# Three 32-byte pads that shift which half of a 64-byte line matmul operands start in

## The chip, the cores and the metric

The kernel runs on one core of a Trainium2 chip. The metric is the device time of one launch in microseconds (us). Three runs of the kernel before took 3115.22, 3119.87 and 3125.04 us; their median is 3119.87 us. The profile shows one more execution, engine by engine: PE is TensorE's matmuls, PEld its weight loads, DVE is VectorE, ACT is ScalarE, POOL is GpSimd, SP issues most DMAs.

## The reference, cut to what matters

One transformer block on 2048 tokens of width 1024, all in float32. The block modulates a layer norm of x, projects it to 6144 columns, runs a convolution branch and a bidirectional retention branch with 4 heads, mixes the two, projects again and normalises. Then come 16 experts, each of which picks 256 tokens:

```python
xe = jax.vmap(lambda hb, ib: hb[ib])(h, idx)
he = jax.nn.silu(jnp.einsum('becd,edf->becf', xe, w_gate)) * jnp.einsum('becd,edf->becf', xe, w_up)
ye = jnp.einsum('becf,efd->becd', he, w_down) * gates[..., None].astype(h.dtype)
```

The matrices `w_gate`, `w_up` and `w_down` are 1024 x 1024 for each expert, so the experts hold most of the arithmetic and most of the weights.

## The kernel before

Nearly every product is made by `mm3` (lines 86 to 89). An operand is kept as two float32r tiles, a high part and a remainder, which `split` (lines 77 to 84) writes: ACT copies the source to the high part (line 80) and DVE subtracts it from the source (line 81). `mm3` then issues three matmuls, high by high, high by low and low by high. The first argument of a matmul streams through TensorE as the moving operand, the second is loaded as the stationary operand. In the trace a matmul is named out<-moving,stationary; so `mm<-xeT,sg` has the tokens `xeT` moving and the expert's weights `sg` stationary, and `mm<-sd,heT` has the weights `sd` moving and the activations `heT` stationary. A matmul with an activation moving has 256 columns here, one with a weight moving mostly 512.

SBUF tiles live in pools that lie one behind the other in each partition, in the order in which the pools are opened: `const`, `wp`, `sm`, and behind them pools that come and go with the stages (`ip`, `hp`, `cvp`, `evp` for the input projections, `rpa` and `rp` for retention and output projection, `ep` for the experts). Within a pool the slots lie in the order in which their tags are first used, and each slot is rounded up to a multiple of 32 bytes. So a slot starts either at byte 0 or at byte 32 of a 64-byte line. `wp` has four `raw` slots (DMA destinations) and 24 slots with tag `w`, all of 4096 bytes; `wp` starts at byte 20480, so all of them start at 0. The pools behind `sm` start at 136960, also at 0. In `ep` come `g2r` (4096 bytes), `kio` (672 bytes, an odd number of 32s) and `idx` (128 bytes), so `heT`, both `xeT` slots, the 2 KB work tiles and `ye` start at 32, while `xe` starts at 0.

Which operand starts where, in the kernel before (moving, stationary):

| matmuls (out<-moving,stationary) | what | moving at | stationary at |
|---|---|---|---|
| `mm<-xeT,sg` | experts, gate and up, 256 columns | 32 | 0 |
| `mm<-sd,heT` | experts, down, 512 columns | 0 | 32 |
| `mm<-hT,sU` | input projection U, 256 columns | 0 | 0 |
| `mm<-sK,hT` and with sQ, sV, sG, sGA, sGB | the other input projections, 512 columns | 0 | 0 |
| `ro<-sw,oTs`, `mm<-sw,yTs`, `mm<-sw,ats` | output projections, 512 columns | 0 | 0 |
| `o<-SS,qws`, `o<-vsr,ats`, `u<-vs,kd`, `ub<-vsr,kd` | retention, 256 columns | 0 | 0 |

`make_hT` (line 256) puts the transposed tokens `hT` of the pairs 0, 1, 5 and 6 in the `hp` pool and those of the pairs 2, 3, 4, 7 and of the context in `w` slots (line 258). In retention `kTs`, `qTs` and `qws` lie in `w` slots, `SS`, `vsr`, `oTs`, `yTs` and nearly all `ats` in `rpa` and `rp`. The order of the work is written out by hand in program order; SP's queue issues the weight loads, and a `raw` slot is loaded again when both of its splits have read it.

Of the kernel before, what the change touches and what calls it, by code (L numbers as in the profile page):

```python
# [9 lines left out]
F32 = mybir.dt.float32  # L10
# [8 lines left out]
DRAM = bass.MemoryType.DRAM  # L19

P = 128
# [7 lines left out]
CAP = 256  # L29
# [13 lines left out]
def body(ctx: ExitStack, tc: tile.TileContext, x, ctxt, cc, w_ada, b_row, b_col, w_in, conv_w, conv_b,  # L43
# [3 lines left out]
    V, A, G, T = nc.vector, nc.scalar, nc.gpsimd, nc.tensor  # L47
# [4 lines left out]
    pp = ctx.enter_context(tc.tile_pool(name="pp", bufs=1, space=PSUM))  # L52
    dr = ctx.enter_context(tc.tile_pool(name="dr", bufs=1, space=DRAM))

    def dram(name, shape, dt=F32):
        return dr.tile(shape, dt, name=name, tag=name)

# [30 lines left out]
        T.matmul(ps, s[0], m[1], start=False, stop=False)  # L88
        return T.matmul(ps, s[1], m[0], start=False, stop=stop_)  # L89

# [1 line left out]
    def cload(name, src, shape, dt=F32, eng=None):  # L92
        t = const.tile(shape, dt, name=name)
        (eng or nc.gpsimd).dma_start(t, src)
# [25 lines left out]
    CB, SB, GB, WB = dect[:, 5], dect[:, 6], dect[:, 7], dect[:, 8:10]  # L120
    wr = const.tile([P, KD, 32], F32, name="wr")

# [1 line left out]
    d_kr = [dram(f"d_kr{t}", [P, 512]) for t in range(NT)]  # L124
    d_kT = [dram(f"d_kT{t}", [P, 512]) for t in range(NT)]
    d_qT = [dram(f"d_qT{t}", [P, 512]) for t in range(NT)]
# [15 lines left out]
    pows, exps = [None], [None]  # L142

    def ln_scale(src, nchunk, heads=1, eps=EPS, fin=True):
        """src [P, nchunk*w] -> rstd, -mean*rstd as [P, heads]"""
        w = src.shape[-1] // nchunk
        n = nchunk // heads
        st = sm.tile([P, nchunk, 6], F32, name="st", tag="st", bufs=4)
        for i in range(nchunk):
            V.bn_stats(st[:, i], src[:, i * w:(i + 1) * w])  # L150
        mv = sm.tile([P, heads, 2], F32, name="mv", tag="mv", bufs=4)
        for h in range(heads):
            V.bn_aggr(mv[:, h], st[:, h * n:(h + 1) * n])
        if not fin:
            rs = sm.tile([P, 1], F32, name="rs1", tag="rs1", bufs=4)
            V.tensor_scalar(rs, mv[:, 0, 1:2], eps, None, op0=ALU.add)  # L156
            pows[0] = G.tensor_tensor(rs, rs, mhalf[:, :1], ALU.pow)  # L157
            return rs, mv
        return ln_fin(mv, heads, eps)
# [9 lines left out]
        for j in range(4):  # L169
            T.transpose(ps[:, j * P:(j + 1) * P], src[:, (k0 + j) * P:(k0 + j + 1) * P], ident)  # L170

    # ======================= input projections =======================
    inp = ExitStack()
    ip = inp.enter_context(tc.tile_pool(name="ip", bufs=1))
    hp_ = inp.enter_context(tc.tile_pool(name="hp", bufs=1))
# [74 lines left out]
    ring = {}  # L250

    def make_hT(pid, src, t0, which):
        """pair of token tiles: modulated LN, transposed, split"""
        tag = "h" if pid in (0, 1, 5, 6) else "w"
        tiles = []
        for kk in range(4):
            if tag == "h":
                tiles.append(hp_.tile([P, 2, 2, 2 * P], F32R, name=f"hT{pid}_{kk}", tag="h", bufs=8))
            else:
                tiles.append(wslot(f"hT{pid}_{kk}", [P, 2, 2, 2 * P]))  # L260
        for t in range(2):
            xt = ip.tile([P, D], F32, name="xt", tag="t4k", bufs=3)
            nc.sync.dma_start(xt, src[(t0 + t) * P:(t0 + t + 1) * P])
            rs = ln_scale(xt, 2)
            A.activation(xt, xt, AF.Identity, scale=rs[:, 0], bias=rs[:, 1])
            for hf in range(2):
                ps = tr_ps()
                transpose4(xt, hf * 4, ps)
                hf32 = t2k("hf32")
                for j in range(4):  # L270
                    k = hf * 4 + j
                    cj = slice(j * P, (j + 1) * P)
                    if j % 2:
                        A.activation(hf32[:, cj], ps[:, cj], AF.Identity,
                                     scale=modc[:, 1, k, which:which + 1], bias=modc[:, 0, k, which:which + 1])
                    else:
                        V.tensor_scalar(hf32[:, cj], ps[:, cj],
                                        modc[:, 1, k, which:which + 1], modc[:, 0, k, which:which + 1],
                                        op0=ALU.mult, op1=ALU.add)
                for q in range(2):  # L280
                    dst = tiles[hf * 2 + q]
                    split(dst[:, :, 0, t * P:(t + 1) * P], dst[:, :, 1, t * P:(t + 1) * P],
                          hf32[:, q * 256:(q + 1) * 256].rearrange("p (k c) -> p k c", k=2))
        ring[pid] = tiles
# [5 lines left out]
        return tl[:, k % 2, 0, t * P:(t + 1) * P], tl[:, k % 2, 1, t * P:(t + 1) * P]  # L290

    def load_w(src, ks, scale=None, res=None):
        """rows of 128 of [n, 1024] -> slabs[half][k]"""
        res = [[], []] if res is None else res
        for k in ks:
            r = raw("rw", [P, D])
            nc.sync.dma_start(r, src[k * P:(k + 1) * P])
            for n in range(2):
                s = wslot("sw", [P, 2, 512])
                split(s[:, 0], s[:, 1], r[:, n * 512:(n + 1) * 512], scale=None if scale is None else scale[:, k:k + 1])  # L300
                res[n].append((s[:, 0], s[:, 1]))
        return res
# [25 lines left out]
    st = {}  # L328

    def rope(ps, t, kq):  # L330
        """ps [P, 512] psum -> rotated f32 pieces written to dst"""
        cs = ip.tile([P, 2, 64], F32, name="cs", tag="cs", bufs=2)
        nc.scalar.dma_start(cs, k_rope[kq, t])
        a = t2k("ra")
        b = t2k("rb")
        pv = ps.rearrange("p (h d) -> p h d", d=64)
        V.tensor_tensor(a.rearrange("p (h d) -> p h d", d=64), pv, cs[:, 0:1].to_broadcast([P, 8, 64]), ALU.mult)
        V.tensor_tensor(b.rearrange("p (h d) -> p h d", d=64), pv, cs[:, 1:2].to_broadcast([P, 8, 64]), ALU.mult)
        a4 = a.rearrange("p (h e d) -> p h e d", e=2, d=64)
        b4 = b.rearrange("p (h e d) -> p h e d", e=2, d=64)  # L340
        return a4, b4
# [243 lines left out]
    inp.close()  # L585


    # ======================= retention =======================
    ret = ExitStack()
    rpa = ret.enter_context(tc.tile_pool(name="rpa", bufs=1))  # L590
    rp = ret.enter_context(tc.tile_pool(name="rp", bufs=1))
# [16 lines left out]
        return s  # L608

    def T_split(src, name):  # L610
        """[P, 1024] token-major -> transposed hi/lo tiles"""
        tl = []
        for hf in range(2):
            ps = tr_ps()
            transpose4(src, hf * 4, ps)
            s = hlT(name)
            split(s[:, 0], s[:, 1], ps)
            tl.append(s)
        return lambda k: (tl[k // 4][:, 0, (k % 4) * P:(k % 4 + 1) * P], tl[k // 4][:, 1, (k % 4) * P:(k % 4 + 1) * P])
# [99 lines left out]
    w_conv_s = load_w(w_conv, range(4))  # L719
    ret_b(0, T_split(prev, "oTs"))  # L720

    # ======================= output projection, LN, router =======================
    def row_const(name, src, off=0, plus1=False):
        if name == "l1b":
            t = rpa.tile([P, D], F32, name=name, tag="tabr", bufs=1)
# [109 lines left out]
                hTs = []  # L835
    ret.close()

    # ======================= expert choice: top CAP tokens of each expert =======================
    moe = ExitStack()
    ep = moe.enter_context(tc.tile_pool(name="ep", bufs=1))  # L840
    def tk(name, w, dt=F32, bufs=1):
# [10 lines left out]
    nc.scalar.dma_start(kio, k_iota)  # L852
    iota16, tokid, blk, iota128 = kio[:, 0:16], kio[:, 16:32], kio[:, 32:40], kio[:, 40:168]
    idx = ep.tile([P, NE * 2], U32, name="idx")

    def gu_slabs(src, f2, ahead=False):
        res = [[], []]
# [30 lines left out]
    for i in range(14, -1, -1):  # L888
        cnt = tk("cnt", 3, BF16, 2)
        for j in range(3):  # L890
            junk = e2k("junk")
            junk = junk[:, :128].bitcast(BF16) if i >= 8 else junk[:, :256]
            V.tensor_scalar(junk, seg16 if i >= 8 else seg, cand[:, j + 1:j + 2].bitcast(F32), 0.0,
                            op0=ALU.is_ge, op1=ALU.add, accum_out=cnt[:, j:j + 1])
        pc = u_ps("cnt")
        cmm = T.matmul(pc[:, 0:3], sameb, cnt, start=True, stop=True)
        if i < 14:
            with tc.issue_after(cmm.ins):
                pump(1, g2fill)
        hits = tk("hits", 3, F32, 2)  # L900
        dig = tk("dig", 1, F32, 2)
        if i > 0:
            nx = tk("nx", 4, I32, 2)
            V.tensor_tensor(nx, cand[:, 0:1].to_broadcast([P, 4]), digit[:, i - 1], ALU.bitwise_or)
        else:
            nx = cand[:, 0:1].to_broadcast([P, 4])
        V.tensor_scalar(hits, pc[:, 0:3], CAP - 0.5, 0.0, op0=ALU.is_ge, op1=ALU.add, accum_out=dig)
        cand = tk("cand", 4, I32, 2)
        if i >= 4:
            # at most 24 significant bits: exact in float32  # L910
            V.scalar_tensor_tensor(cand, dig.to_broadcast([P, 4]), float(1 << 2 * i), nx, op0=ALU.mult, op1=ALU.add)
        else:
            digi = tk("digi", 1, I32, 2)
            V.tensor_scalar(digi, dig, float(1 << 2 * i), None, op0=ALU.mult)
            V.tensor_tensor(cand, digi.to_broadcast([P, 4]), nx, ALU.bitwise_or)
# [61 lines left out]
        g0 = 2 if gq == 0 else 0  # L977
        nc.sync.dma_start(idx[:, gq * 8 + g0:(gq + 1) * 8], d_idx.rearrange("(h g p) o -> h p (g o)", h=4, p=P)[gq][:, g0:])

    # list of expert 0, in the layout that its gathers read  # L980
    pin0 = pin.rearrange("p (a s e) -> p a s e", a=2, s=8)[:, :, :, 0]
    pt = tk("pt", 32, I32)
    V.tensor_scalar(pt[:, 0:16].rearrange("p (s a) -> p a s", a=2), pin0, P - 1, None, op0=ALU.bitwise_and)
# [23 lines left out]
    V.tensor_copy(pabf, pab)  # L1007


    # ======================= experts =======================  # L1010
    def x_prep(e):
        xeT = ep.tile([P, KD, 2, 256], F32R, name="xeT", tag="xeT", bufs=2)
        gts = []
# [138 lines left out]
    moe.close()  # L1152


# [1 line left out]
def layout(**inp):  # L1156
    f=lambda n: np.ascontiguousarray(inp[n])
    w_in=inp['w_in'][0]
# [60 lines left out]
```

## Time and profile before

| | before |
|---|---|
| median of 3 runs | 3119.87 us (3115.22 to 3125.04) |
| profiled execution, span | 3120.2 us |
| PE busy | 2992.0 us, 96% of the span |
| DVE busy | 2142.9 us, 69% |
| ACT busy | 1170.9 us, 38% |
| mean granted TensorE clock | 0.979 |

Of the profiled execution the records give the span from the first to the last instruction; no time outside it is recorded. A matmul's duration in the records runs from its issue to its modelled end and overlaps the next one, so the cost of a matmul in a dense stream is read from the distance between the starts of neighbours, here called the spacing, and not from its duration.

### The profile page before, as it was taken

Reading aid. Unit: us, or ns where it says so; the run is one execution under the profiler, and the core shown is the slowest. Engines: PE = TensorE matmul, PEld = TensorE weight load, DVE = VectorE, ACT = ScalarE, POOL = GpSimd, SP = SyncE. Lnnn points to the kernel's source line nnn. Section 1 sums busy time; section 2 is a strip of 40 time slices with the busy share of each in tenths; the row PEclk is TensorE's granted clock in tenths of the full one; section 3 lists DMA queues with packets and bytes.
Section 4 is the critical chain, followed back from the end, with each engine's and each line's share of the span. In section 5 each row is a group of like instructions: output and inputs, shape, how many; then the busy total and the mean of one; then the engine's idle time right before and its main releaser. Section 6 shows DMA issues by size and latency. Waiting matters only on the chain.

```text
span 3120.2 us, 47124 instructions
## 1 busy us (share of the span) xinstructions
PE 2992.0 (96%) x17897; PEld 2599.5 (83%) x17897; DVE 2142.9 (69%) x3964; ACT 1170.9 (38%) x2182; POOL 338.2 (11%) x294
## 2 busy tenths in 40 slices
PE   6999999999999999899999995999999999999897
PEld 3988877789888887788888881999999999998886
DVE  4366777452669985888877777566666666588686
ACT  4323123252232233555421112555555555444342
POOL 2100000000000000111101114100000000011131
PEclk8999999999999999899999996999999999999998
DMA  6244355332442334666754444666766666588774
GB/s 238 82 147 169 135 172 174 121 109 87 170 180 90 118 117 143 208 205 210 238 198 151 145 139 158 199 204 213 212 218 215 210 211 211 175 274 270 243 257 162
DMA packets 195043, 560.22 MB, mean 180 GB/s; under 512 B 29064, under 2 KB 44328, under 8 KB 194816
## 3 DMA queue, kind: packets, MB, share of 16 engines
q1 hardware_dynamic: 174880, 503.68, 48.4%
q0 software_dynamic: 13456, 47.84, 6.0%
q10 hardware_dynamic: 6480, 5.70, 0.6%
q8 instruction: 140, 2.29, 0.3%
q14 instruction: 87, 0.71, 0.1%
HBM read 429.24 MB, written 127.89 MB: 179 GB/s over the span
## 4 chain that ended last, share of the span: by engine, by line
PE 85%; DMA 6%; DVE 4%; issue 2%; ACT 2%; POOL 1%; SPq 0%; POOLq 0%; DVEq 0%; ACTq 0%
PE mm L87 24%; PE mm L89 23%; PE mm L88 23%; PE tr L170 2%; PE ro L87 2%; PE ro L89 2%; PE ro L88 2%; DMA rg<-w_gate 1%; DMA d_acc<-ye,idx 1%; DMA rg<-w_up 1%; PE ada L206 1%; PE o L87 1%; PE o L88 1%; PE o L89 1%; DVE sd L81 1%
## 5 line engine op out<-in xcount | busy, mean ns | idle before, releaser
L89 PE MATMUL mm<-xeT,sg 128*128 128x256 f32 x2048 | 575.8, 281 | 14.2 <-DVE sg L81 9.9
L87 PE MATMUL mm<-xeT,sg 128*128 128x256 f32 x2048 | 576.9, 282 | 2.4 <-ACT sg L80 2.2
L88 PE MATMUL mm<-xeT,sg 128*128 128x256 f32 x2048 | 574.5, 281 | 0.0
L81 DVE TENSOR_TENSOR sg<-rg,sg 128x512 fp32r<-128x512 f32 x488 | 328.1, 688 | 218.7 <-ACT sg L80 217.5
L80 ACT ACTIVATE sg<-rg 128x512 fp32r<-128x512 f32 x512 | 312.2, 629 | 338.9 <-PE mm L89 207.2
L89 PEld LDWEIGHTS mm<-xeT,sg 128*128 128x128 f32 x2048 | 387.1, 189 | 16.6 <-DVE sg L81 14.3
L87 PEld LDWEIGHTS mm<-xeT,sg 128*128 128x128 f32 x2048 | 387.4, 189 | 4.2 <-ACT sg L80 3.5
L88 PEld LDWEIGHTS mm<-xeT,sg 128*128 128x128 f32 x2048 | 387.3, 189 | 0.7
L451 DVE SCALAR_TENSOR_TENSOR cacc<-yw,cvw,cacc 128x384 f32<-128x384 f32 (+1 forms) x600 | 376.2, 640 | 8.7
L81 DVE TENSOR_TENSOR sd<-rd,sd 128x512 fp32r<-128x512 f32 x256 | 171.4, 686 | 82.7 <-ACT sd L80 82.0
L87 PE MATMUL mm<-sd,heT 128*128 128x512 f32 x512 | 204.1, 399 | 6.6 <-ACT heT L80 6.6
L80 ACT ACTIVATE sd<-rd 128x512 fp32r<-128x512 f32 x256 | 157.1, 628 | 130.3 <-PE mm L89 82.9
L89 PE MATMUL mm<-sd,heT 128*128 128x512 f32 x512 | 204.5, 399 | 0.8 <-DVE heT L81 0.8
L88 PE MATMUL mm<-sd,heT 128*128 128x512 f32 x512 | 203.6, 398 | 0.0
L164 POOL TENSOR_TENSOR rs<-rs,mhalf 128x1 f32<-128x1 f32 (+1 forms) x50 | 37.0, 742 | 1311.3 <-DVE rs L163 1213.1
L88 PE MATMUL mm<-hT,sU 128*128 128x256 f32 x512 | 146.8, 287 | 3.0 <-DVE hT L81 2.9
L87 PE MATMUL mm<-hT,sU 128*128 128x256 f32 x512 | 146.8, 288 | 2.8 <-ACT hT L80 2.8
L89 PE MATMUL mm<-hT,sU 128*128 128x256 f32 x512 | 146.5, 287 | 0.0
L157 POOL TENSOR_TENSOR rs<-rs,mhalf 128x1 f32<-128x1 f32 x58 | 83.4, 1438 | 482.7 <-DVE rs L156 464.2
L87 PEld LDWEIGHTS mm<-sd,heT 128*128 128x128 f32 x512 | 97.1, 190 | 30.5 <-ACT heT L80 8.3
L428 ACT ACTIVATE gs<-mm 128x512 f32<-128x512 f32 x96 | 54.9, 597 | 173.5 <-PE mm L89 149.4
L89 PEld LDWEIGHTS mm<-sd,heT 128*128 128x128 f32 x512 | 96.9, 189 | 26.1 <-DVE heT L81 2.8
(352 smaller groups left out, 7121.8 us busy)
## 6 DMA issues: line engine op xcount, KB each, us to landing
rg<-w_gate SPq DMA_DIRECT2D x128, 512.0 KB, 4.2
rg<-w_up SPq DMA_DIRECT2D x128, 512.0 KB, 3.9
rd<-w_down SPq DMA_DIRECT2D x128, 512.0 KB, 4.8
wa<-w_ada SPq DMA_DIRECT2D x40, 512.0 KB, 4.8
d_v<-vs SPq DMA_DIRECT2D x32, 512.0 KB, 3.2
vsr<-d_v SPq DMA_DIRECT2D x32, 512.0 KB, 4.4
xt<-x SPq DMA_DIRECT2D x16, 512.0 KB, 3.7
rU<-w_in SPq DMA_DIRECT2D x16, 512.0 KB, 4.3
```

Of the source, the lines that this page charges most:

```text
L80: A.activation(hi, src, AF.Copy)
L81: eng.tensor_tensor(lo, src, hi.bitcast(F32), ALU.subtract)
L87: T.matmul(ps, s[0], m[0], start=start, stop=False)
L88: T.matmul(ps, s[0], m[1], start=False, stop=False)
L89: return T.matmul(ps, s[1], m[0], start=False, stop=stop_)
L157: pows[0] = G.tensor_tensor(rs, rs, mhalf[:, :1], ALU.pow)
L164: G.tensor_tensor(rs[:, 0], rs[:, 0], mhalf[:, :heads], ALU.pow)
L170: T.transpose(ps[:, j * P:(j + 1) * P], src[:, (k0 + j) * P:(k0 + j + 1) * P], ident)
L206: T.matmul(ps[32 * jj:32 * jj + 32, :], crep[:, k], wt[:, j * 512:(j + 1) * 512], start=k == 0, stop=k == KD - 1)
L428: A.activation(s, ps, AF.Sigmoid)
L451: V.scalar_tensor_tensor(acc[:, :n], y[:, tap:tap + n], cvw[:, cgp, tap:tap + 1], acc[:, :n], op0=ALU.mult, op1=ALU.add)
```

## The change

Three tiles of 8 float32 words (32 bytes a partition) are allocated and cleared by a memset on DVE each: one as the first slot of `wp`, one as the first slot of `sm`, and one in `ep` behind `idx`. The remaining hunks of the diff take out comments and docstrings.

```diff
     dr = ctx.enter_context(tc.tile_pool(name="dr", bufs=1, space=DRAM))
+    for pool in (wp, sm):
+        V.memset(pool.tile([P, 8], F32, name="pad", tag="pad", bufs=1), 0.0)
...
     idx = ep.tile([P, NE * 2], U32, name="idx")
+    V.memset(ep.tile([P, 8], F32, name="pad", tag="pad", bufs=1), 0.0)
```

By the sizes above this moves every `raw` and `w` slot by 32 bytes, to byte 32 of a line. The slots of `sm` and all pools behind it move by 64 bytes and keep their half. In `ep` everything behind `idx` moves by another 32: `heT`, `xeT`, the work tiles and `ye` go to byte 0, `xe` goes to byte 32.

| matmuls | moving at, before to after | stationary at, before to after |
|---|---|---|
| `mm<-xeT,sg` | 32 to 0 | 0 to 32 |
| `mm<-sd,heT` | 0 to 32 | 32 to 0 |
| `mm<-hT,sU` | half of them 0, half 0 to 32 | 0 to 32 |
| other input projections | 0 to 32 | half of them 0, half 0 to 32 |
| `ro<-sw,oTs`, `mm<-sw,yTs`, `mm<-sw,ats` | 0 to 32 | 0 |
| `o<-SS,qws` | 0 | 0 to 32 |
| `o<-vsr,ats`, `u<-vs,kd`, `ub<-vsr,kd` | 0 | 0 |

## Rows read from the trace of the kernel before

**Rows 1.** The page: busy time of each engine (us, share of the span, instructions), and the chain of work that ended last, by engine.

```profile
PE 2992.0 (96%) x17897; PEld 2599.5 (83%) x17897; DVE 2142.9 (69%) x3964; ACT 1170.9 (38%) x2182; POOL 338.2 (11%) x294
...
PE 85%; DMA 6%; DVE 4%; issue 2%; ACT 2%; POOL 1%; SPq 0%; POOLq 0%; DVEq 0%; ACTq 0%
```

**Rows 2.** The timeline of PE around four dense stretches: for each, its first and its last matmul (start us, duration us). Between first and last, both counted, lie 192 matmuls of `mm<-hT,sU`, 144 of `mm<-sGA,hT`, 96 of `mm<-sd,heT` and 192 of `mm<-xeT,sg`, and nothing else on PE.

```profile
112.96 0.28 PE L88 MATMUL mm<-hT,sU 128*128 128x256 f32 x1
...
135.86 0.28 PE L87 MATMUL mm<-hT,sU 128*128 128x256 f32 x1
...
1060.58 0.39 PE L87 MATMUL mm<-sGA,hT 128*128 128x512 f32 x1
...
1092.99 0.39 PE L89 MATMUL mm<-sGA,hT 128*128 128x512 f32 x1
...
2006.34 0.40 PE L87 MATMUL mm<-sd,heT 128*128 128x512 f32 x1
...
2028.51 0.40 PE L89 MATMUL mm<-sd,heT 128*128 128x512 f32 x1
...
2028.75 0.28 PE L87 MATMUL mm<-xeT,sg 128*128 128x256 f32 x1
...
2051.04 0.27 PE L89 MATMUL mm<-xeT,sg 128*128 128x256 f32 x1
```

**Rows 3.** The same four stretches by windows: us, then busy us and instructions of PE, PEld, DVE, ACT and POOL, the granted TensorE clock, the DMA engines' busy share, GB/s. Order: U, GA, down, gate and up.

```profile
112.95:135.90 22.95, 22.95 (x194) 22.95 (x193) 6.03 (x13) 5.18 (x12) 0.00 (x0) 1.00 0.22 70
...
1060.57:1093.10 32.53, 32.53 (x145) 26.94 (x144) 28.67 (x54) 3.70 (x7) 0.00 (x0) 1.00 0.31 95
...
2006.33:2028.75 22.42, 22.42 (x99) 18.07 (x97) 13.61 (x21) 10.75 (x17) 0.00 (x0) 1.00 0.63 190
...
2028.74:2051.20 22.46, 22.46 (x195) 22.45 (x193) 14.41 (x24) 12.93 (x27) 3.48 (x2) 1.00 0.82 232
```

**Rows 4.** Groups of PE instructions by line and form: shapes, count, busy us, mean ns of one, idle us before. Of each `mm3` group the second of its three lines stands here (L88); L87 and L89 have the same count. L170 is a transpose.

```profile
L88 PE MATMUL mm<-xeT,sg 128*128 128x256 f32 x2048 | 574.5, 281 | 0.0
L88 PE MATMUL mm<-sd,heT 128*128 128x512 f32 x512 | 203.6, 398 | 0.0
L88 PE MATMUL mm<-hT,sU 128*128 128x256 f32 x512 | 146.8, 287 | 3.0 <-DVE hT L81 2.9
L88 PE MATMUL ro<-sw,oTs 128*128 128x512 f32 x256 | 101.0, 394 | 0.0
L88 PE MATMUL mm<-sV,hT 128*128 128x512 f32 x256 | 99.9, 390 | 0.0
L88 PE MATMUL mm<-sGB,hT 128*128 128x512 f32 x256 | 99.9, 390 | 0.0
L88 PE MATMUL mm<-sG,hT 128*128 128x512 f32 x256 | 99.8, 390 | 0.0
L88 PE MATMUL mm<-sGA,hT 128*128 128x512 f32 x256 | 99.7, 389 | 0.0
L88 PE MATMUL mm<-sw,yTs 128*128 128x512 f32 x256 | 99.5, 390 | 0.0
L88 PE MATMUL mm<-sw,ats 128*128 128x512 f32 x128 | 50.0, 391 | 0.0
L88 PE MATMUL mm<-sQ,hT 128*128 128x512 f32 x128 | 49.9, 390 | 0.0
L88 PE MATMUL mm<-sK,hT 128*128 128x512 f32 x128 | 49.9, 390 | 0.0
L88 PE MATMUL o<-SS,qws 128*128 128x256 f32 x128 | 36.1, 287 | 0.0
L170 PE MATMUL tr<-ident,xe 128*128 128x128 f32 x256 | 34.5, 284 | 2.9 <-DMA xe<-d_h,idx 2.8
L88 PE MATMUL att<-qTs,kTs 128*128 128x128 f32 x64 | 18.4, 288 | 2.8 <-DVE qTs L81 2.8
L170 PE MATMUL tr<-ident,ybl 128*128 128x128 f32 x128 | 17.6, 274 | 0.0
L88 PE MATMUL mm<-sV,hTc 128*128 128x512 f32 x32 | 12.5, 390 | 0.0
L88 PE MATMUL mm<-sK,hTc 128*128 128x512 f32 x16 | 6.2, 389 | 0.0
```

**Rows 5.** Groups of weight loads by line and form, one of GA's kind and one of the down kind: count, busy us, mean ns of one, idle us before.

```profile
L88 PEld LDWEIGHTS mm<-sG,hT 128*128 128x128 f32 x256 | 48.1, 188 | 9.6
...
L88 PEld LDWEIGHTS mm<-sd,heT 128*128 128x128 f32 x512 | 97.0, 189 | 22.6
```

**Rows 6.** The last 420 us by windows, columns as in rows 3.

```profile
2700.00:2850.00 150.00, 144.45 (x1013) 133.24 (x1013) 102.37 (x165) 60.44 (x111) 24.77 (x17) 0.99 0.72 233
2850.00:3000.00 150.00, 140.84 (x982) 128.96 (x981) 114.52 (x187) 64.85 (x120) 27.12 (x20) 0.99 0.78 253
3000.00:3120.00 120.00, 96.71 (x599) 86.21 (x598) 83.04 (x135) 40.82 (x73) 30.20 (x24) 0.92 0.59 197
```

**Rows 7.** The memset of an 8-word tile on DVE, by tile: count, duration ns minimum/median/maximum, start.

```profile
L109 DVE MEMSET mhalf<- x1: 65/65/65, 0.8 to 0.8; 128x8 f32 x1
```

## The prediction, made before the changed kernel ran

> **What bounds the kernel now.** I read the page first. PE is busy for 2992.0 of 3120.2 us, and the chain of waits that ended last runs over PE for 85% of its length [rows 1]. No other engine comes near: DVE, the next one, is busy 69%. So a change in how fast neighbouring matmuls follow each other goes to the end nearly in full, and a change on DVE, ACT or POOL hardly at all. The change adds no arithmetic and moves no step; what it alters is the address at which operands start. So the question is whether PE's spacing depends on that, and the kernel before answers in part, because its operands already start in both halves of a 64-byte line.
>
> The second view is therefore the timeline of PE, at four dense stretches [rows 2]. Spacing is last start less first start, over the count less one:
> - U, moving at 0, stationary at 0, 256 columns: 135.86 - 112.96 = 22.90 us over 191 = 119.9 ns.
> - GA, moving at 0, stationary at 0, 512 columns: 1092.99 - 1060.58 = 32.41 us over 143 = 226.6 ns.
> - down, moving at 0, stationary at 32, 512 columns: 2028.51 - 2006.34 = 22.17 us over 95 = 233.4 ns.
> - gate and up, moving at 32, stationary at 0, 256 columns: 2051.04 - 2028.75 = 22.29 us over 191 = 116.7 ns.
>
> The third view, windows over the same stretches, says what the differences are not. [...] The load on the other engines does not order them either: GA has DVE busy 28.67 of 32.53 us and is the faster of the two 512-column streams, and gate and up, with the busiest DMA (0.82), is the faster of the two 256-column ones. What the pairs differ in is the halves. The weight load itself takes the same in both kinds, 188 and 189 ns [rows 5], so it is the stream that gives.
>
> With 512 columns a pair in different halves is 6.8 ns slower than a pair in the same half; with 256 columns it is 3.2 ns faster. I read the four numbers by two laws. In the same half a matmul costs its columns and a fixed part: 226.6 - 119.9 = 106.7 ns for 256 columns more, so 13.2 ns are fixed. In different halves it costs by columns alone: 233.4 / 512 = 0.456 and 116.7 / 256 = 0.456 ns a column. The equality of these two is what I build on: it comes out although in one pair it is the moving operand that lies at 32, and in the other the stationary one. So I take it that what counts is whether the two lie in the same half, and not which of them lies where.
>
> **The change part by part.**
> - Gate and up: 3 x 2048 = 6144 matmuls [rows 4] go from (32, 0) to (0, 32). Still different halves: 0 by the law. No row has (0, 32) with 256 columns; the bounds are below.
> - Down: 3 x 512 = 1536 matmuls [rows 4] go from (0, 32) to (32, 0): 0 by the law.
> - Of the other input projections, sV, sGB, sG and sGA with 256 and sQ and sK with 128 a line [rows 4] make 3 x (4 x 256 + 2 x 128) = 3840 matmuls. Half of them have `hT` in `hp` and so go from the same half to different halves: 1920. The output projections, 256 + 256 + 128 a line, go there whole: 3 x 640 = 1920. Together 3840 x (233.4 - 226.6) = 3840 x 6.8 ns = +26.1 us.
> - U: 3 x 512 = 1536, half of which, 768, go to different halves; so do all 3 x 128 = 384 of `o<-SS,qws` [rows 4]. 1152 x (116.7 - 119.9) = -3.7 us.
> - From (0, 0) to (32, 32) go 1920 of the input projections, 3 x (32 + 16) = 144 of the context, 768 of U and 3 x 64 = 192 of `att` [rows 4]: 0 by the law. No row shows two operands at 32 in a dense stream. The nearest rows are the three other pairs, so each could shift by anything from -3.2 to +6.8 ns; 3024 matmuls give -9.7 to +20.6 us.
> - Transposes of `xe` and `ybl`, 256 + 128 [rows 4], get their stationary operand in the other half. With 128 columns no row shows different halves; by the same two ends it is -1.2 to +2.6 us. I take 0.
> - Splits: each reads a `raw` slot and writes a `w` slot, both now at 32. No row shows what a half does to DVE or ACT. They are covered: while PE is full in gate and up, DVE is busy for 14.41 and ACT for 12.93 of 22.46 us [rows 3], so either could be half as slow again before PE waits. I take 0.
> [...]
> - Three memsets at 65 ns [rows 7] = 0.2 us on DVE. The first two stand before any input has landed, the third before the experts' selection, ahead of nothing that it could hold up for longer than itself. By the sizes the shift by 32 in `ep` makes no slot overlap an earlier tile that it did not overlap before, so no new release is waited for.
>
> Sum: 26.1 - 3.7 + 0.2 = +22.6 us. Against the profiled execution that is 3120.2 + 22.6 = 3142.8 us. The median of the runs lies 0.3 us below that execution's span, so I carry it over unchanged: about 3142 us.
>
> **The rivals.**
> First, it matters which operand lies at 32, and the two effects add: a stationary operand at 32 costs 6.8 ns (GA to down), a moving one at 32 saves 3.2 ns (U to gate and up). For it speaks that each step is a measured one; against it that the equal cost per column is then a coincidence. Then gate and up go from 116.7 to 126.7: 6144 x 10.0 = +61.4; down goes the other way, 1536 x -10.0 = -15.4; the 3840 with 512 columns -12.3; the 1152 with 256 columns +7.8. Sum +41.5, with the pairs at (32, 32) at 0: 3162 us; with these at +3.6 each, 3173.
>
> Second, on the other side: the width decides who is short. With 256 columns stream and weight load are equally long, with 512 the load is over early; so different halves could help the short stream whichever way round, and the 233.4 ns could come from the stationary operand at 32 in a long stream alone. Then gate and up stay, down falls to 226.6 - 3.2 = 223.4 (1536 x -10.0 = -15.4), the 3840 save 3.2 each (-12.3), the 1152 save 3.7: -31.4, or 3089 us. If down's 233.4 has a cause other than the halves and stays, -16.0, or 3104 us. Its place is the down stream; it decides from the point where that stream falls under 226.6 ns with `sd` at 32. For it: both rows with 256 columns favour different halves. Against it: then the only 512-column row is the exception.
>
> Third, nothing changes: the differences come from the stages and not from the halves, and every stream keeps its spacing, 3120 us. For it: the four streams stand in different stages. Against it: U and GA, in different stages, agree on one law, and the windows name no other difference. [...]
>
> **How the numbers follow.** The forecast gets 0.33, the additive rival 0.25, the faster rival 0.30 (its two prices together), no change 0.12. About 0.3% (9 us) is what a measurement of this kernel can tell from no change. Slower than that come out the forecast and the additive rival, 0.57 with a little lost to the edge; faster 0.30; within it 0.13. The range goes from 3090, which takes in most of the faster rival, to 3173, the additive one's dearer price; under 2 in 10 is left out. The forecast's own range is 3132 to 3163, from its unshown pairs at (32, 32).
>
> **What would show it.** By the timeline of PE in the changed kernel: gate and up at 116.7 and down at 233.4 as before, `mm<-sw,yTs` at 233 instead of 226.6, U's first pair at 116.7 and its third at 120. Gate and up at 127 would make the additive rival right, `mm<-sw,yTs` and down at 223 the faster one. [...]

## The result, and the profile after

The changed kernel takes 3156.54 us (median of 4 runs, 3152.03 to 3161.21) against 3120.71 us for the kernel before in 4 runs (3115.22 to 3125.04). The ratio is 1.0121, with a 95% interval of 1.0102 to 1.0139: slower by 1.0 to 1.4%. The profiled execution has a span of 3155.7 us, 35.5 more than before. The prediction was 3142 us with 3090 to 3173 around it, and 3132 to 3163 for its own case. Direction and range held; the sum came out 13 us short of the span, and the cause of that is more than a size. That the time lies inside 3132 to 3163 is luck: those ends were made from the pairs at (32, 32), which kept their spacing, and what was missing came from gate and up, priced at nothing.

In the page of the changed kernel these lines answer to [rows 1]. Line numbers are 4 higher than before: `mm3` is at L91 to L93, `split` at L84 and L85.

```profile
PE 3033.1 (96%) x17897; PEld 2620.1 (83%) x17897; DVE 2143.2 (68%) x3967; ACT 1171.5 (37%) x2182; POOL 339.6 (11%) x294
...
PE 83%; DMA 7%; DVE 5%; issue 3%; ACT 2%; POOL 1%; SPq 0%; POOLq 0%; DVEq 0%; ACTq 0%
```

PE has the same 17897 instructions and is busy 41.1 us longer. DVE, ACT and POOL move by 1.4 us at most, so the change is in how fast PE works, and the next view is PE's timeline at dense stretches, as in [rows 2]. Each stretch is shown by its first and last matmul (start us, duration us). Their counts are 147 for U with its tokens in `hp`, 169 for U with its tokens in `w` slots, 48 for `mm<-sw,yTs`, 96 for down and 192 for gate and up.

```profile
708.36 0.28 PE L91 MATMUL mm<-hT,sU 128*128 128x256 f32 x1
...
725.40 0.28 PE L93 MATMUL mm<-hT,sU 128*128 128x256 f32 x1
...
728.14 0.28 PE L92 MATMUL mm<-hT,sU 128*128 128x256 f32 x1
...
748.30 0.28 PE L92 MATMUL mm<-hT,sU 128*128 128x256 f32 x1
...
1616.95 0.40 PE L91 MATMUL mm<-sw,yTs 128*128 128x512 f32 x1
...
1627.92 0.39 PE L93 MATMUL mm<-sw,yTs 128*128 128x512 f32 x1
...
2030.74 0.39 PE L91 MATMUL mm<-sd,heT 128*128 128x512 f32 x1
...
2053.00 0.39 PE L93 MATMUL mm<-sd,heT 128*128 128x512 f32 x1
...
2053.23 0.28 PE L91 MATMUL mm<-xeT,sg 128*128 128x256 f32 x1
...
2076.16 0.28 PE L93 MATMUL mm<-xeT,sg 128*128 128x256 f32 x1
```

The spacings are 17.04 / 146 = 116.7 ns for U from `hp`, 20.16 / 168 = 120.0 for U from `w` slots, 10.97 / 47 = 233.4 for `mm<-sw,yTs`, 22.26 / 95 = 234.3 for down and 22.93 / 191 = 120.1 for gate and up. The first three are what the prediction named. Gate and up are not: 120.1 in place of 116.7, in the largest group of the kernel. Down is 0.9 ns above its 233.4.

Windows that part the span at the same events of both kernels show where the 35.5 us lie: up to the first U matmul, up to the first gate matmul of expert 0, experts 0 to 10, and experts 11 to 15 with the end. Columns are as in [rows 3]. First the kernel before:

```profile
0.00:46.00 46.00, 21.40 (x85) 5.30 (x85) 10.54 (x33) 12.08 (x23) 10.48 (x20) 0.93 0.83 284
46.00:1957.20 1911.20, 1847.04 (x9842) 1549.02 (x9842) 1365.04 (x2735) 587.51 (x1145) 184.80 (x169) 0.98 0.46 153
1957.20:2725.70 768.50, 767.23 (x5510) 718.19 (x5510) 474.83 (x725) 409.51 (x720) 60.78 (x45) 1.00 0.68 208
2725.70:3120.20 394.50, 356.30 (x2465) 327.02 (x2463) 292.51 (x474) 161.83 (x296) 82.09 (x61) 0.97 0.73 239
```

The same four stretches of the changed kernel:

```profile
0.00:47.10 47.10, 22.32 (x85) 6.57 (x85) 10.28 (x35) 12.08 (x23) 10.48 (x20) 0.88 0.82 277
47.10:1980.30 1933.20, 1869.14 (x9841) 1550.25 (x9842) 1364.41 (x2736) 588.02 (x1145) 185.90 (x169) 0.97 0.45 151
1980.30:2762.50 782.20, 780.96 (x5511) 731.64 (x5511) 475.87 (x725) 409.67 (x720) 58.74 (x45) 1.00 0.67 205
2762.50:3155.70 393.20, 360.69 (x2465) 331.68 (x2463) 292.69 (x474) 161.69 (x296) 84.51 (x61) 0.97 0.73 240
```

| stretch | span, after less before | PE busy, after less before | predicted |
|---|---|---|---|
| up to the first U matmul | +1.1 | +0.9 | +0.2 |
| up to expert 0 | +22.0 | +22.1 | +22.4 (26.1 - 3.7) |
| experts 0 to 10 | +13.7 | +13.7 | 0 |
| experts 11 to 15, end | -1.3 | +4.4 | 0 |

Two things are to be read here. All before the experts came as predicted. That it fits within a microsecond is partly luck: the stretch up to expert 0 takes 1926.6 to 1933.8 us in the four kernels with the weights at 32 (the changed kernel, e2, e6, e7) and 1907.7 to 1911.2 in the four with them at 0 (the kernel before, e1, e3, e8), so one execution of each tells the difference only to some 5 us. In the experts, which were priced at nothing, PE works 18.1 us longer; the 13.7 in experts 0 to 10 reach the end, and the 4.4 in the last stretch do not. There PE idled 394.5 - 356.3 = 38.2 us before and idles 393.2 - 360.7 = 32.5 us now: the slower matmuls stand where PE would have waited.

### The profile page after: what moved, and what is told of

Read it like the earlier page. It is cut to its first block, busy times and chain, and to the rows that moved or that the text cites. A ratio compares the mean times of both kernels' runs of the same rounds, so it can differ in the third digit from the quotient of the medians.

```text
span 3155.7 us, 47127 instructions
## 1 busy us (share of the span) xinstructions
PE 3033.1 (96%) x17897; PEld 2620.1 (83%) x17897; DVE 2143.2 (68%) x3967; ACT 1171.5 (37%) x2182; POOL 339.6 (11%) x294
## 4 chain that ended last, share of the span: by engine, by line
PE 83%; DMA 7%; DVE 5%; issue 3%; ACT 2%; POOL 1%; SPq 0%; POOLq 0%; DVEq 0%; ACTq 0%
PE mm L91 23%; PE mm L93 23%; PE mm L92 23%; PE tr L174 3%; PE ro L91 2%; PE ro L93 2%; PE ro L92 2%; DMA d_acc<-ye,idx 1%; DMA rd<-w_down 1%; DMA rg<-w_gate 1%; DVE sg L85 1%; PE ada L210 1%; PE o L91 1%; PE o L92 1%; PE o L93 1%
## 5 line engine op out<-in xcount | busy, mean ns | idle before, releaser
L93 PE MATMUL mm<-xeT,sg 128*128 128x256 f32 x2048 | 582.3, 284 | 11.3 <-DVE sg L85 8.3
L91 PE MATMUL mm<-xeT,sg 128*128 128x256 f32 x2048 | 582.2, 285 | 2.3 <-ACT sg L84 2.2
L85 DVE TENSOR_TENSOR sg<-rg,sg 128x512 fp32r<-128x512 f32 x488 | 328.4, 688 | 225.4 <-ACT sg L84 220.0
L84 ACT ACTIVATE sg<-rg 128x512 fp32r<-128x512 f32 x512 | 312.1, 629 | 343.7 <-PE mm L93 212.1
L93 PEld LDWEIGHTS mm<-xeT,sg 128*128 128x128 f32 x2048 | 386.3, 189 | 13.7 <-DVE sg L85 13.7
L91 PEld LDWEIGHTS mm<-xeT,sg 128*128 128x128 f32 x2048 | 387.4, 189 | 3.8 <-ACT sg L84 3.2
L85 DVE TENSOR_TENSOR sd<-rd,sd 128x512 fp32r<-128x512 f32 x256 | 171.9, 687 | 90.5 <-ACT sd L84 89.7
L84 ACT ACTIVATE sd<-rd 128x512 fp32r<-128x512 f32 x256 | 157.2, 628 | 137.5 <-PE mm L93 90.6
L91 PE MATMUL mm<-sd,heT 128*128 128x512 f32 x512 | 204.0, 398 | 3.9 <-ACT heT L84 3.9
L93 PE MATMUL mm<-sd,heT 128*128 128x512 f32 x512 | 203.9, 398 | 0.8 <-DVE heT L85 0.8
L91 PE MATMUL mm<-hT,sU 128*128 128x256 f32 x512 | 146.6, 287 | 2.3 <-ACT hT L84 2.3
L93 PE MATMUL mm<-hT,sU 128*128 128x256 f32 x512 | 146.4, 286 | 0.0
L91 PEld LDWEIGHTS mm<-sd,heT 128*128 128x128 f32 x512 | 96.7, 189 | 28.2 <-ACT heT L84 5.7
L93 PEld LDWEIGHTS mm<-sd,heT 128*128 128x128 f32 x512 | 96.8, 189 | 26.3 <-DVE heT L85 2.9
```

The source lines that it names most:

```text
L84: A.activation(hi, src, AF.Copy)
L85: eng.tensor_tensor(lo, src, hi.bitcast(F32), ALU.subtract)
L91: T.matmul(ps, s[0], m[0], start=start, stop=False)
```

## The experiments

After these two traces the theory was still the law of halves with a flaw in one place; its rivals were that the position of one operand alone decides, or that only a wider address than the 64-byte line explains gate and up. Four kernels ran first: three that keep a part of the change, and one that measures streams by themselves.

**Only the activations, apart from each other (e1_heT0).** From the kernel before, with 32 bytes behind `idx` and 32 more behind `heT`, so that `heT` lies at 0 of a 64-byte line and `xeT` still at 32. Weights are at 0.

```diff
     idx = ep.tile([P, NE * 2], U32, name="idx")
+    V.memset(ep.tile([P, 8], F32, name="pad", tag="pad", bufs=1), 0.0)
...
         wg2.append(ep.tile([P, 4, D], F32, name="wg2", tag=tag, bufs=bufs))
+        if i == 0:
+            V.memset(ep.tile([P, 8], F32, name="pad2", tag="pad2", bufs=1), 0.0)
```

> The kernel before with heT alone moved to byte 0 of its line; xeT moves by a whole 64 bytes and stays at 32, all weights stay at 0. If the halves decide: gate and up stay at 116.7 ns, down goes from (0, 32) to (0, 0) and from 233.3 to 226.6 ns; 1536 x 6.7 = 10.3 us less, about 3110 us. If down's spacing belongs to its stage: 233.3 ns and 3120 us.

Measured: 3133.22 us (8 runs), ratio 1.0037 (1.0024 to 1.0051). PE's timeline of this kernel, first and last matmul of one stretch of down (96) and one of gate and up (192):

```profile
2005.32 0.39 PE L87 MATMUL mm<-sd,heT 128*128 128x512 f32 x1
...
2027.48 0.39 PE L89 MATMUL mm<-sd,heT 128*128 128x512 f32 x1
...
2027.71 0.28 PE L87 MATMUL mm<-xeT,sg 128*128 128x256 f32 x1
...
2050.63 0.28 PE L89 MATMUL mm<-xeT,sg 128*128 128x256 f32 x1
```

Down has 22.16 / 95 = 233.3 ns with both operands in the same half, where the law wants 226.6. Gate and up have 22.92 / 191 = 120.0 ns with the operands in the same halves as in the kernel before, where they took 116.7. So neither case of the expectation came: the halves fall, for the same two halves give two spacings, and so does a spacing that belongs to the stage, for gate and up changed theirs where they stand.

**Only the weights (e2_weights_only).** The pads of `wp` and `sm`, without the one in `ep`.

```diff
+    for pool in (wp, sm):
+        V.memset(pool.tile([P, 8], F32, name="pad", tag="pad", bufs=1), 0.0)
```

> Only the first two pads of the change (weights to 32), none in ep: xeT and heT stay at 32, so gate and up and down are pairs (32, 32). If the halves decide: gate and up 120.0 ns, down 226.6 ns, the rest as in the changed kernel; that is the changed kernel less 1536 x 7.5 = 11.5 us, about 3145 us. If in the experts a weight at 32 costs something of its own: gate and up 120 or above, down over 226.6 ns and nearer to 3157 us.

Measured: 3140.55 us (4 runs), ratio 1.0068 (1.0048 to 1.0088). One stretch of gate and up (192 matmuls) in its timeline:

```profile
2045.68 0.28 PE L90 MATMUL mm<-xeT,sg 128*128 128x256 f32 x1
...
2068.18 0.28 PE L92 MATMUL mm<-xeT,sg 128*128 128x256 f32 x1
```

That is 22.50 / 191 = 117.8 ns, a value that neither case of the expectation had; down has 233.4.

**Only the experts' pool (e3_ep_only).** The pad behind `idx` alone.

```diff
     idx = ep.tile([P, NE * 2], U32, name="idx")
+    V.memset(ep.tile([P, 8], F32, name="pad", tag="pad", bufs=1), 0.0)
```

> Only the third pad (xeT and heT to 0, weights stay at 0). If the halves decide: gate and up (0, 0) at 120.0 ns, down (0, 0) at 226.6 ns, all else as in the kernel before; 6144 x 3.3 = +20.3 us, of which some 14 reach the end as in the changed kernel, less 10.3 us, so 3124 to 3131 us. If what gate and up lost in the change was the weights' move to 32: 116.7 ns and about 3110 us.

Measured: 3122.87 us (10 runs), ratio 1.0001 (0.9990 to 1.0013), no difference. The same stretch in its timeline:

```profile
2027.32 0.28 PE L87 MATMUL mm<-xeT,sg 128*128 128x256 f32 x1
...
2049.82 0.28 PE L89 MATMUL mm<-xeT,sg 128*128 128x256 f32 x1
```

Again 22.50 / 191 = 117.8 ns, and down again 233.4, which neither case of the expectation had. Here both experts' operands lie 32 bytes lower than in e2, and the spacings are equal. That points at the difference of the two addresses. It also shows that the parts do not add: 18.3 us for the weights alone and 0.6 for `ep` alone, 35.8 for both.

So I worked the addresses out again from the sizes of the pools, this time modulo 256, in place of 64 (e4 and e7 below bear on that unit). The distance is the stationary address less the moving one, modulo 256.

| kernel | gate and up (moving, stationary), distance | ns | down (moving, stationary), distance | ns |
|---|---|---|---|---|
| before | (32, 0) 224 | 116.7 | (0, 32) 32 | 233.4 |
| after | (128, 32) 160 | 120.0 | (32, 128) 96 | 234.3 |
| e1_heT0 | (96, 0) 160 | 120.0 | (0, 64) 64 | 233.3 |
| e2_weights_only | (96, 32) 192 | 117.8 | (32, 96) 64 | 233.4 |
| e3_ep_only | (64, 0) 192 | 117.8 | (0, 64) 64 | 233.4 |

In the changed kernel `xeT` and `heT` have moved by 32 + 32 + 32 = 96 bytes, two pads in front of the pool and one in it. Equal distances stand beside equal spacings throughout. The output projections of the changed kernel, (32, 64), have distance 32 and 233.4 ns, as down had before; U from `hp`, (64, 32), has 224 and 116.7, as gate and up had before.

**Streams by themselves (e4_streams).** A kernel that issues 96 matmuls after each other from two float32r tiles, at chosen byte offsets `om` (moving) and `os` (stationary), with no other work beside them; it computes nothing of the block.

```python
for a, b in ((0, 0), (0, 1), (1, 0)):
    T.matmul(ps[:, :n], st[:, os + s[a]:os + s[a] + P], mv[:, om + m[b]:om + m[b] + n], ...)
```

> Bare streams of 96 matmuls on TensorE with no other engine at work, 256 and 512 columns, moving and stationary each at 0, 16, 32 and 48 bytes in a line, and some at 64 to 320; it computes nothing of the block. If the halves decide: with 512 columns (0, 0) and (32, 32) at 226.6 and (0, 32) and (32, 0) at 233.4 to 234.2 ns; with 256 columns (0, 0) and (32, 32) at 120.0 and (32, 0) at 116.7. The pair (0, 32) with 256 columns and the steps of gate and up comes at 120.0 here if the addresses make what the changed kernel shows, at 116.7 if the load of the experts' other engines makes it; and if a larger unit than 64 bytes counts, the streams with the moving operand 64, 128, 256 and 320 bytes further differ from each other.

Its timeline shows each stream as one row: start, length of the whole stream, name and count. The names are n for 256 columns and w for 512, then moving and stationary offset, where a is 0, c is 32, g is 128, i is 256 and k is 320. The spacing is the length less the last matmul's own 0.28 us, over 95.

```profile
52.57 11.52 PE L51 MATMUL n_ac<-mv,st 128*128 128x256 f32 x96
...
120.23 11.36 PE L51 MATMUL n_ca<-mv,st 128*128 128x256 f32 x96
...
576.55 11.68 PE L51 MATMUL n_gc<-mv,st 128*128 128x256 f32 x96
...
588.07 11.53 PE L51 MATMUL n_ic<-mv,st 128*128 128x256 f32 x96
...
599.43 11.37 PE L51 MATMUL n_kc<-mv,st 128*128 128x256 f32 x96
```

The moving operand at 0, 128 and 320 with the stationary one at 32 is the same pair of halves three times, and gives 118.3, 120.0 and 116.7 ns. `n_gc`, the addresses of the changed kernel's gate and up, has its 120.0 with all other engines at rest; `n_ca`, those of the kernel before, has 116.6. So for these two pairs the difference is the addresses and not the stage. And `n_ac` and `n_gc`, whose moving operands lie 128 bytes apart, differ, so the unit is more than 128 bytes; `n_ac` and `n_ic`, which lie 256 apart, have 118.3 and 118.4, and so the other two pairs of streams that lie 256 apart agree (116.6 and 116.7 both times).

**A map in steps of 16 bytes (e5_map).** The same kernel over 128 pairs of offsets for each width, letters a to p for 0 to 240, and at the end five pairs bare, beside ACT and DVE splits (eng), and beside DMA (dma). It computes nothing of the block either.

> Bare streams again, with the moving operand at the byte address where xeT lies in the changed kernel less 64 and the stationary one where the first w slot lies less 32, and both shifted in steps of 16 bytes up to 240; it computes nothing of the block. If a 64-byte line decides, a shift of either operand by 64 changes no spacing. If a larger unit does, the 512-column stream at (0, 64) is near 233.3 ns, as down in the run with only the third pad, and returns to 226.7 at a shift of 128 or 256. The last fifteen streams repeat five pairs alone, beside splits on ACT and DVE, and beside DMA loads: if the other engines' load made gate and up 120 ns in the changed kernel, (64, 32) is 116.7 alone and 120 beside them; if the addresses do, 120 in all three.

Rows of its timeline, 72 matmuls each, the last three 144:

```profile
166.79 8.56 PE L59 MATMUL n_ca<-mv,st 128*128 128x256 f32 x72
...
302.35 8.64 PE L59 MATMUL n_ea<-mv,st 128*128 128x256 f32 x72
...
438.40 8.80 PE L59 MATMUL n_ga<-mv,st 128*128 128x256 f32 x72
...
455.54 8.32 PE L59 MATMUL n_gc<-mv,st 128*128 128x256 f32 x72
...
506.19 8.36 PE L59 MATMUL n_ha<-mv,st 128*128 128x256 f32 x72
...
591.45 8.80 PE L59 MATMUL n_ic<-mv,st 128*128 128x256 f32 x72
...
1118.09 16.53 PE L59 MATMUL w_aa<-mv,st 128*128 128x512 f32 x72
...
1150.78 16.95 PE L59 MATMUL w_ac<-mv,st 128*128 128x512 f32 x72
...
1217.86 17.03 PE L59 MATMUL w_ag<-mv,st 128*128 128x512 f32 x72
...
3284.25 16.48 PE L59 MATMUL bare_ea<-mv,st 128*128 128x256 f32 x144
...
3368.57 17.14 PE L59 MATMUL eng_ea<-mv,st 128*128 128x256 f32 x144
...
3453.56 17.14 PE L59 MATMUL dma_ea<-mv,st 128*128 128x256 f32 x144
```

With 256 columns `n_ic`, the pair (128, 32), has (8.80 - 0.28) / 71 = 120.0 ns and `n_ga`, (96, 0) with the same distance 160, the same; `n_ca` has 116.6; `n_ha`, (112, 0) at distance 144, has 113.8. With 512 columns `w_aa` has (16.53 - 0.39) / 71 = 227.3, `w_ac` 233.2 and `w_ag`, distance 96, 234.4. These are the kernels' own values.

The expectation took (64, 32) for the changed kernel's pair of gate and up. Modulo 256 that pair is (128, 32), and (64, 32) has the distance 224 of the kernel before; it took 116.6 ns alone and 117.8 beside splits and beside DMA, which is neither outcome named. The 512-column stream at (0, 64) has 233.2 ns as expected, but a shift by 128, to (0, 192), gives 228.9 and not 226.7.

What the whole map says: with 512 columns and the moving operand at a multiple of 32, the spacing goes with the distance. It is 226.6 to 226.9 ns at 0, 16 and 240 (227.3 in `w_aa`), 228.9 to 232.0 at 80, 176 and 192, 234.4 at 96, and 233.1 to 233.5 elsewhere, but for one stream each at 128 and 208 (232.4 and 231.8). With 256 columns the distance decides most of it. At 160 all eight pairs have 119.9 to 120.0; at 0 those with operands at multiples of 32 have 119.9 to 120.1; at 224 five of eight have 116.6; at 144 six of eight have 113.2 to 114.1. At 64 and 192, with operands at multiples of 32, a stream takes 113.2 to 113.4 or 117.7 to 117.9, and the addresses do not fix which: the pair (64, 0) has (16.48 - 0.28) / 143 = 113.3 ns in `bare_ea` and (8.64 - 0.28) / 71 = 117.7 in `n_ea`, where nothing ran beside it either. Beside splits or DMA it has 117.9, but that their work is the cause is not shown. The second half of `dma_ea`, as a row of the timeline and as a window with its columns as in [rows 3], keeps the spacing when the DMA is over:

```profile
3461.82 8.88 PE L59 MATMUL dma_ea<-mv,st 128*128 128x256 f32 x74
...
3462.00:3470.50 8.50, 8.50 (x74) 8.50 (x74) 0.00 (x0) 0.00 (x0) 0.00 (x0) 1.00 0.00 0
```

That is (8.88 - 0.28) / 73 = 117.8 ns with every other engine idle and a DMA share of 0.00. In e2 and e3 the one stretch of 174 gate matmuls in expert 0 ran at 113.3 and all others at 117.8. The kernel before has two spacings as well: most of its gate and up runs at 116.7, but some stretches at 117.8, such as 191 matmuls from 2404.79 to 2427.17 us.

**Only the distance of gate and up restored (e6_pad224).** The changed kernel, with the third pad 224 bytes long instead of 32: `xeT` and `heT` go to 64, so gate and up have distance 224 and down 32, as before the change; the first two pads stay.

```diff
-    V.memset(ep.tile([P, 8], F32, name="pad", tag="pad", bufs=1), 0.0)
+    V.memset(ep.tile([P, 56], F32, name="pad", tag="pad", bufs=1), 0.0)
```

> The changed kernel with the pad in ep 224 bytes long instead of 32, so that xeT and heT lie at byte 64 of a 256-byte unit instead of 128; 0 in a 64-byte line as before. If the distance of the stationary from the moving operand within 256 bytes decides (gate and up 160 to 224, down 96 to 32): gate and up 116.7 ns, down 233.4 ns; 6144 x 3.3 + 1536 x 0.9 = 21.7 us less PE time, of which the last experts hide about a third, so about 3141 us. If 64-byte lines decide: 120.0 ns, 234.2 ns and 3156 us.

Measured: 3145.47 us (5 runs), ratio to the kernel before 1.0062 (1.0043 to 1.0082). One stretch of gate and up (192) in its timeline:

```profile
2049.40 0.28 PE L91 MATMUL mm<-xeT,sg 128*128 128x256 f32 x1
...
2071.69 0.27 PE L93 MATMUL mm<-xeT,sg 128*128 128x256 f32 x1
```

22.29 / 191 = 116.7 ns: the term that the prediction lost is undone, and the time is 1.0062 of the kernel before where the prediction's 22.6 us would be 1.0072. Experts 0 to 10 take 766.7 us by their window, against 768.5 before and 782.2 in the changed kernel:

```profile
1979.13:2745.82 766.69, 765.42 (x5510) 716.25 (x5510) 475.10 (x725) 410.33 (x720) 60.58 (x45) 1.00 0.69 209
```

**The unit (e7_pad288).** The same with 288 bytes, 256 more than in the change: `[P, 72]` in place of `[P, 8]`.

> The changed kernel with the pad in ep 288 bytes long, so that all in ep lies 256 bytes further. If 256 bytes are the unit: nothing changes, gate and up 120.0 ns, down 234.2 ns, about 3156 us. If the unit is larger: another spacing.

Measured, in one run: 3150.72 us. One stretch of gate and up (192) in its timeline:

```profile
2044.40 0.28 PE L91 MATMUL mm<-xeT,sg 128*128 128x256 f32 x1
...
2067.32 0.28 PE L93 MATMUL mm<-xeT,sg 128*128 128x256 f32 x1
```

Gate and up have 22.92 / 191 = 120.0 ns and down 234.2, as in the changed kernel. A shift by 256 changes no spacing, one by 192 (e6) does; the 5.8 us by which this run is shorter than the changed kernel are taken up at the end.

**The map used (e8_xeT112_heT0).** The kernel before without the change's pads; instead tiles in `ep` and an offset of four words in the slots of `xeT` put `xeT` at 112 (distance 144 to weights at 0) and `heT` at 0 (distance 0).

```diff
+    gap("ga", 16)
+    for i, (tag, w) in enumerate((("xeTa", 4100), ("heT", 4096))):
...
-        xeT = ep.tile([P, KD, 2, 256], F32R, name="xeT", tag="xeT", bufs=2)
+        xeT = ep.tile([P, 4100], F32R, name="xeT", tag="xeT" + "ab"[e % 2], bufs=1)
+        xeT = xeT[:, 4:].rearrange("p (k h c) -> p k h c", k=KD, h=2)
```

> The kernel before with the first words of xeT's slots skipped so that xeT lies at byte 112 of a 256-byte unit (distance 144) and heT at 0 (distance 0); the weights stay at 0. If distance decides and the bare streams carry over: gate and up 113.3 ns instead of 116.7, down 226.7 instead of 233.3; 6144 x 3.4 + 1536 x 6.7 = 31 us less PE time, of which the last experts hide about a third: about 3098 us. If the load of the other engines takes the fast pattern away, as it took 113.3 to 117.8 at (64, 0): gate and up 116.7 to 117.8 and 3110 to 3117 us.

Measured: 3101.17 us (5 runs), ratio to the kernel before 0.9928 (0.9911 to 0.9944); it is faster than both kernels. Down (96) and gate and up (192) in its timeline:

```profile
2002.42 0.39 PE L87 MATMUL mm<-sd,heT 128*128 128x512 f32 x1
...
2023.98 0.39 PE L89 MATMUL mm<-sd,heT 128*128 128x512 f32 x1
...
2024.21 0.28 PE L87 MATMUL mm<-xeT,sg 128*128 128x256 f32 x1
...
2045.89 0.28 PE L89 MATMUL mm<-xeT,sg 128*128 128x256 f32 x1
```

Down has 21.56 / 95 = 226.9 ns, gate and up 21.68 / 191 = 113.5, with all engines at work; so the expectation's second case, in which their load takes the fast spacing away, did not come. The last two of the four windows, experts 0 to 10 and the rest, show where this counts:

```profile
1954.30:2702.90 748.60, 747.35 (x5510) 704.61 (x5510) 474.65 (x725) 410.36 (x720) 58.04 (x45) 1.00 0.70 214
2702.90:3099.60 396.70, 353.82 (x2465) 326.69 (x2463) 292.60 (x474) 161.80 (x296) 94.50 (x61) 0.95 0.73 238
```

Experts 0 to 10 take 748.6 us, 19.9 less than before; the rest takes 396.7, 2.2 more, with PE idle for 42.9. The profiled execution is shorter by another 2.9 us ahead of the experts; the last section has their place. The last five experts last about as long at 113.5, 116.7 and 120.0 ns a gate matmul (396.7, 394.5 and 393.2 us), so there the matmul's spacing is not what bounds them.

## Why the prediction came out as it did

**The bound and the method held.** PE's spacing was the quantity that changed; clock, DVE, ACT and DMA were not. The granted clock is 1.00 in all four stretches of [rows 3], in which PE is never idle, and in experts 0 to 10 of both kernels, so neither the clock nor a wait makes these spacings; the weight loads of gate and up have a mean of 189 to 190 ns, near [rows 5], and the pads' memsets are lost in DVE's total (2142.9 and 2143.2 us). That the loads' own records stay the same does not say, as the prediction had it, that the stream alone gives way: in e5, with the other engines at rest, the step from `w_aa` to `w_ac` moves only the stationary operand by 32 bytes and takes the spacing from 227.3 to 233.2 ns.

**Terms that held.** The 3840 matmuls of 512 columns at +6.8 ns and the 1152 of 256 columns at -3.2 ns were to make +22.4 us ahead of the experts; PE is busy 22.1 us longer there, and the two spans differ by 22.0. The pairs that went from (0, 0) to (32, 32), priced at nothing between wide bounds, kept 120.0 ns (U from `w` slots). Splits at nothing held too, and the transfers, for which the sum has no term, kept their rate: the last stretch has a DMA share of 0.73 and 239 or 240 GB/s in both.

**The step that failed** is the law itself where it prices "gate and up: still different halves: 0 by the law", and with it "down: 0 by the law". Gate and up went from 116.7 to 120.0 ns, 6144 x 3.3 = +20 us of PE, and down from 233.4 to 234.3, 1536 x 0.9 = +1.4. By the windows the two together are 18.1 us and not some 21; what makes the difference was not traced. The law had been read from four streams whose distances are 0, 0, 32 and 224 modulo 256, and for those it is right. All terms that came true end at one of these three distances, which nothing in the law had asked for; that part of its success is luck. Gate and up and down alone were moved to others, 160 and 96, because I had counted how far `ep` moved modulo 64 only: the two pads in front move the pool by 64, which keeps the half but not the distance. What I built on, equal cost per column in both kinds of different halves, was a coincidence: in the changed kernel both pairs lie in different halves as well, at 120.0 / 256 = 0.469 and 234.3 / 512 = 0.458 ns a column. The bounds of the two terms were announced ("the bounds are below") but taken up only in the rivals, so the forecast's own range held nothing for its largest group.

**What softened it.** Of the 18.1 us of PE in the experts, the 4.4 in experts 11 to 15 do not reach the end, for PE idles 5.7 us less there. Without that the miss would have been larger. The row for it, [rows 6], stood ahead of the prediction, and the sum drew nothing from it.

**The rivals.** The additive one is nearest in time (3162) but is wrong in every number that makes it up: gate and up did not go to 126.7, and down and `mm<-sw,yTs` did not fall to 223. The faster one falls by `mm<-sw,yTs` at 233.4. Its premise on the loads is what [rows 3] has: with 256 columns they are busy as long as the stream (22.45 of 22.46 us in gate and up), with 512 they are not (18.07 of 22.42 us in down). No change falls by the ratio, 1.0121.

**Still open.** Why the period is 256 bytes (e4, e7), and what chooses between two spacings at distances 64, 192 and 224, no run shows. The pair (128, 32) was run bare and in the changed kernel, but not in e5 beside splits or DMA. The map gives the size of the effect, not its mechanism. Better distances for `hT`, `SS` and `vsr`, which stand at 0 in the kernel before, were not tried.

## What to carry to other kernels

Where dense float32r matmuls with a new stationary operand each bound a kernel, the address of a tile is a tuning knob (e8, with gate and up at 113.5 ns and down at 226.9, took 0.9928 of the time before): count the distance between stationary and moving operand modulo 256 for each dense group, by every slot in front of it, and look its spacing up in a map such as e5 before moving a slot; where a distance has two spacings, as 64 has 113.3 and 117.7 ns in e5, reckon with the slower. A pad moves everything behind it in SBUF, so its price is the sum over all groups whose distance changes, and the pads here did not cost the sum of each alone (18.3 us for the weights and 0.6 for `ep`, 35.8 for both). A law read from a few streams holds for the distances that these streams had; price the largest group with a range where its new pair has not been seen.

## What the runs showed of the hardware that I had not expected

- With the distance of the two operands modulo 256 bytes a 256-column float32r matmul goes between 113.3 and 120.0 ns, and a 512-column one with its moving operand at a multiple of 32 between 226.7 and 234.4, at a granted clock of 1.00 in the experts' windows.
- At some distances the same pair has more than one spacing without any work beside it: (64, 0) has 113.3 and 117.7 ns in e5, and (16, 0) has 113.3 in e4 and 118.7 and 116.6 in e5. A dense stretch mostly keeps to one: in the kernel before, eleven stretches of 192 gate and up matmuls between 2028.75 and 2748.02 us have 116.6 or 116.7 ns in both halves.

Executions also differ by a few microseconds at one place ahead of the experts. Between the first matmul of `mm<-sw,ats` and the first of `mm<-sw,yTs`, PE waits 2.5 us for DVE's `yb` in the changed kernel, and the granted clock of that stretch is 0.88 in its window:

```profile
1568.70:1598.00 29.30, 26.30 (x105) 20.68 (x106) 11.02 (x19) 5.26 (x10) 0.00 (x0) 0.88 0.43 141
```

In e7 PE did not wait there; the window of the same stretch has the clock at 1.00 and the work takes 24.0 us:

```profile
1565.30:1589.30 24.00, 23.99 (x108) 18.74 (x106) 9.67 (x16) 4.79 (x10) 0.00 (x0) 1.00 0.52 183
```

The kernel before had the wait too (28.2 us at 0.94), so the comparison of the two profiles holds only 1.1 us from this, while some 5 us of e7's shorter time are from here. The change is not the cause: e1, e3 and e8, which differ from the kernel before only in the experts' pool, opened later, take 24.1 to 25.1 us there at 1.00, and 4.1 us of e8's shorter execution come from this place.
